# Decay attention's bias as two rows of the second score product, its mask in the reduction, and weights loaded into their final tiles, in a hybrid S5 / decay-attention layer

## The chip, the cores and the metric

The kernel runs on one core of one Trainium2 chip. The metric is the device time of one execution in microseconds (us), here the median of three executions; lower is better. TensorE is written PE, VectorE DVE, ScalarE ACT, GpSimd POOL and SyncE SP, as in the profile.

## What is computed

One layer of an encoder over 1024 positions of width 1024: an S5 state-space branch and a decay ("forgetting") attention of 8 heads x 64 side by side, one output projection and a residual; cross-attention to 256 memory tokens; a gated feed-forward. The change touches the decay attention and what follows it. Cut to that:

```python
cum_log_f = jnp.cumsum(jax.nn.log_sigmoid(f_logit), axis=1)          # per head and position
for blk in range(seq // 128):                                        # causal, 128 queries at a time
    q0, k_end = blk * 128, blk * 128 + 128
    s = jnp.einsum('bqhd,bkhd->bhqk', q[:, q0:k_end], k[:, :k_end]) / sqrt(64)
    s = jnp.where(q_pos[:, None] >= k_pos[None, :],
                  s + cum_log_f[q0:k_end, None] - cum_log_f[None, :k_end], -1e30)
    outs.append(softmax(s) @ v[:, :k_end])
x = x + rms_norm(concat(rms_norm(y_ssm), rms_norm(y_fox)) @ w_out)   # w_out: 512 rows for each branch
x = x + rms_norm(softmax(h @ wq @ k_mem.T / 16) @ v_mem @ wo)        # k_mem, v_mem = mem_n @ wkv
```

A row's softmax doesn't change when a constant is added to the row, so only the term of the key, `-cum_log_f[k]`, has to be added.

## The kernel before

Every large product is done as three products in the format fp32r: each operand is split in a high part (ACT rounds it, `split`, line 113) and a low part (DVE subtracts, line 115), and `mm3` (lines 121 to 124) multiplies high x high, high x low and low x high. Work is recorded by Python generators in stages; a scheduler then fixes one order for each engine, and each engine runs its list in that order. So an instruction that waits holds up all that stands behind it on its engine. That goes for SP too, which issues nearly all loads. Tiles come from pools with a fixed number of buffers (tag `a`: 2, `b`: 2, `c`: 3, `e`: 1, `t2`: 3, `raw`: 2, `whl`: 3, `slab`: 16), and a load into a buffer waits until the last reader of what was in it is done.

The stages around the change:

- **Input projections** (`in_proj`, line 869): keys, values, gates and queries, with the S5 recurrence on DVE between them. `qk_tile` writes queries and keys to DRAM (`qk_d`) as a high and a low half, `f_gate` (line 336) the running sum of the log gates (`nc_d`). The value tiles of the second half (`v1`) are spread between the S5 output steps `ssm_out` by the numbers in `V1_AT` (line 38). `ssm_out` (line 635) multiplies with tables `T` that SP loads from `T_d` (line 632).
- **Decay attention** (`fox`, line 705): 64 units, 8 heads x 8 blocks of 128 queries. `prepare` (line 709) loads for a head the query tile `qs` (64 high rows over 64 low rows), the keys `ka` (high keys in both halves of the rows, and low keys in both), and `ncb`, the running sum repeated over 128 partitions. `scores` (line 722) makes up to 1024 columns in a two-bank PSUM tile: for each 512 columns a product with the high keys (line 730) and one with the low keys (line 731), and on the last 128 columns a third one that adds the mask (line 733, a bf16 identity x `maskb`). One DVE instruction (line 737) adds `ncb` and takes the row minimum; ACT exponentiates (739), DVE divides by the row sum (740, 741). `turn` transposes the unit on PE (758), `values` multiplies with v (772). The scores run two units ahead.
- **Fillers** between the units, on the same engines: gated unit of S5 (`glu`), the S5 half of the output projection (`out_ssm`, line 818, to DRAM `t1_d`, which the trace calls t_d), memory keys and values (`mem_load` with `raw<-in_memT`, `mem_tile` with a weight `in_wkv` each, line 966), and the first key matrix of the cross-attention (`build_a`, line 993).
- **Output projection** (lines 1023 to 1082): the attention half of w_out is loaded in four pieces to `raw` and split to four slabs; then a loop over eight row blocks multiplies (PSUM tile x), adds the S5 half `t` (loaded at line 1063, line 1070), squares, normalises and adds x (loaded at 1060, line 1078). The value weights of the cross-attention (`value_weights`) are made between them.
- The cross-attention, the feed-forward (line 1294) and its last product (line 1557) follow.

Of the kernel before, what the change touches and what calls it, by code (L numbers as in the profile page):

```python
# [17 lines left out]
P = 128  # L18
S = 1024
# [18 lines left out]
V1_AT = (3, 1, 1, 1, 1)  # L38
# [14 lines left out]
def layer(ctx: ExitStack, tc: tile.TileContext, a, out):  # L53
# [35 lines left out]
    identb = const.tile([P, P], BF16, name="identb")  # L89
    dve.tensor_copy(identb, ident)  # L90
# [57 lines left out]
    boost = 5000  # L148
    stA, stB, stC = pool, pool, pool
# [4 lines left out]
    def load_w(src, shape, first=0, stage=None):  # L154
        w = tt(stage, [P, D]) if stage else raw([P, D])
        hl = whl([P, 2, D])
        if not first:
            sp.dma_start(out=w, in_=src)
# [23 lines left out]
    nc_d = dram.tile([NH, S], F32, name="nc_d")  # L182
    t1_d = dram.tile([L, NC, D], F32, name="t1_d")
    kv_d = dram.tile([16, P, 256], F32, name="kv_d")
    x1_d = dram.tile([NT, P, D], F32, name="x1_d")
# [150 lines left out]
    def f_gate(ftok):  # L336
        ps = s_ps([P, S])[0:NH]
        for j in range(NT):
            pe.transpose(ps[:, j * P:(j + 1) * P], ftok[:, j], ident)
        f, fl = ps, tt("a", [NH, S])  # L340
        dve.tensor_scalar(out=f, in0=ps, scalar1=fb, scalar2=None, op0=ALU.add)
        f = f.rearrange("p (j c) -> p c j", j=L)
        fc = fl.rearrange("p (c j) -> p c j", j=L)
        act.activation(out=fc, in_=f, func=AF.Abs)
        act.activation(out=fl, in_=fl, func=AF.Exp, scale=-1.0)
        act.activation(out=fl, in_=fl, func=AF.Ln, bias=1.0)
        dve.scalar_tensor_tensor(out=fc, in0=f, scalar=0.0, in1=fc, op0=ALU.min, op1=ALU.subtract)
        dve.tensor_tensor_scan(out=fl, data0=fl, data1=fl, initial=0.0, op0=ALU.add, op1=ALU.min)
        stA.dma_start(out=nc_d, in_=fl)
# [355 lines left out]
    def fox(yf):  # L705
# [3 lines left out]
        def prepare(h):  # L709
            r0 = (h % 2) * 64  # L710
            qs = tt("a", [P, S], F32R)
            ka = slab([P, 2, S])
            ncb = tt("b")
            sp.dma_start(out=ncb, in_=nc_d[h:h + 1, :].broadcast_to([P, S]))
            heads[h] = (qs, ka, ncb)
            q, k = qs.bitcast(F32), ka.bitcast(F32)
            for t in range(2):
                sp.dma_start(out=q[t * 64:t * 64 + 64], in_=qk_d[h // 2, t, r0:r0 + 64])
            for rr in (0, 64):
                sp.dma_start(out=k[rr:rr + 64], in_=qk_d[4 + h // 2, :, r0:r0 + 64].rearrange("t p s -> p t s"))  # L720

        def scores(h, t):
            qs, ka, ncb = heads[h]
            ke = (t + 1) * P
            ps = s_ps([P, S])
            qt = qs[:, t * P:(t + 1) * P]
            for c0 in range(0, ke, 512):
                c1 = min(ke, c0 + 512)
                dg = c1 == ke
                pe.matmul(ps[:, c0:c1], qt, ka[:, 0, c0:c1], start=True, stop=False)  # L730
                pe.matmul(ps[:, c0:c1], qt, ka[:, 1, c0:c1], start=False, stop=not dg)  # L731
                if dg:
                    pe.matmul(ps[:, ke - P:ke], identb, maskb, start=False, stop=True)
            sc = tt("c")
            nlr = sm(3, "nlr")
            nm, l, rl = (nlr[:, i:i + 1] for i in range(3))
            dve.tensor_tensor_reduce(out=sc[:, :ke], in0=ps[:, :ke], in1=ncb[:, :ke], scale=1.0,
                                     scalar=3e38, op0=ALU.add, op1=ALU.min, accum_out=nm)
# [294 lines left out]
    def value_weights(h):  # L1033
        vr = t2t([P, 2, 256])
        sp.dma_start(out=vr, in_=kv_d[8 + 2 * h:8 + 2 * h + 2].rearrange("d p m -> p d m"))
        vh = tt("bebe"[h], [P, 2, 2, 256], F32R)
        split(vh[:, 0], vh[:, 1], vr)
# [3 lines left out]
        for c in range(2):  # L1041
            tiles = [(mt, (x_ps if h == 3 else g_ps)([P, 512])) for mt in range(2)]
            for d in range(2):
                for mt, ps in tiles:
                    ms = slice(mt * P, mt * P + P)
                    mm3(ps, vh[:, 0, d, ms], vh[:, 1, d, ms], wo_[d][0][:, c], wo_[d][1][:, c], d == 0, d == 1)
# [10 lines left out]
    for n, j in enumerate((3, 4, 5, 6, 7, 0, 1, 2)):  # L1057
        ts = slice(j * P, (j + 1) * P)
        xt = tt("c")
        sp.dma_start(out=xt, in_=a["x"][ts, :])  # L1060
        t = tt("aab"[n % 3])
        for i in range(2):
            sp.dma_start(out=t[64 * i:64 * i + 64], in_=t1_d.rearrange("j (k s) d -> s k j d", s=16)[2 * j + i])
# [565 lines left out]
```

## Time and profile before

| | |
|---|---|
| median of 3 runs (lowest, highest) | 1413.33 us (1409.28, 1413.37) |
| profiled execution: its own time, its span | 1414.33 us, 1412.5 us |
| PE, DVE, ACT, POOL busy | 98%, 67%, 46%, 27% of the span |
| granted TensorE clock over the span | 0.992 |
| attention with its fillers | from 235.0 us (first score product) to 489.8 us (last value product starts) |
| output projection and start of the cross-attention | to about 560 us |

PE's busy time overlaps itself where matmuls are pipelined, so a share of busy time says little about how fast products follow each other. What is read below is the start of one product against the start of the next, the gaps in which PE has nothing running, and the granted clock of a stretch: PEclk 0.84 means that TensorE was granted 84% of its full clock in that stretch. Rows of waits name the engine that was late by the semaphore that came last.

### The profile page before, as it was taken

To read this page: it belongs to the slowest core of one execution; us is meant where nothing else is said; L and a number is where in the kernel's file an instruction comes from. 1 tells how busy PE (TensorE), PEld (TensorE's weight loads), DVE (VectorE), ACT (ScalarE), POOL (GpSimd) and SP (SyncE) were. 2 spreads that over 40 slices of the span, in tenths; PEclk is the share of its full clock that TensorE was granted. 3 is DMA by queue.
4 is the path that set the end of the run, shared out by engine and by line. 5 is a ranking of instruction groups with operands and counts; after the bars stand their busy time and mean duration, and the time that the engine had idled before them with its cause. 6 is when DMAs were issued, how large, how long until landed. Compare 5 with 4: busy or idle time off the path is not lost.

```text
span 1412.5 us, 20273 instructions
## 1 busy us (share of the span) xinstructions
PE 1381.8 (98%) x7353; PEld 1163.3 (82%) x7353; DVE 951.9 (67%) x1719; ACT 652.3 (46%) x1289; POOL 379.7 (27%) x430
## 2 busy tenths in 40 slices
PE   9999989999999899999999999999999999999997
PEld 7889889789889677888888788888888888888886
DVE  8949944857567668545467777877776676655566
ACT  7383345766566546433344533333333334544351
POOL 0011110011211043001021367676766661000021
PEclk9999999999999999999999999999999999999999
DMA  6235665267663665024467345554444447955544
GB/s 217 91 108 163 201 220 138 69 200 213 183 180 113 175 194 186 27 75 152 161 202 257 97 176 193 178 187 161 145 158 154 165 150 236 357 196 194 179 164 164
DMA packets 104501, 239.45 MB, mean 170 GB/s; under 512 B 11464, under 2 KB 40136, under 8 KB 104272
## 3 DMA queue, kind: packets, MB, share of 16 engines
q1 hardware_dynamic: 85872, 176.24, 40.0%
q0 software_dynamic: 18528, 61.91, 12.3%
q8 instruction: 58, 0.95, 0.3%
q14 instruction: 43, 0.35, 0.1%
HBM read 169.43 MB, written 77.33 MB: 175 GB/s over the span
## 4 chain that ended last, share of the span: by engine, by line
PE 84%; DVE 7%; issue 3%; DMA 3%; ACT 2%; POOL 0%; SPq 0%; DVEq 0%; ACTq 0%; POOLq 0%
PE x L1294 17%; PE g L1294 13%; PE x L1557 7%; PE g L1557 7%; PE g L122 7%; PE g L124 7%; PE g L123 7%; PE x L123 2%; PE x L124 2%; PE g L758 2%; PE x L122 2%; PE g L772 2%; PE s L730 1%; PE s L731 1%; DMA a<-t_d 1%
## 5 line engine op out<-in xcount | busy, mean ns | idle before, releaser
L1294 PE MATMUL x<-slab,op 128*128 128x512 f32 x984 | 233.2, 389 | 0.5 <-DVE op L115 0.5
L1294 PEld LDWEIGHTS x<-slab,op 128*128 128x128 f32 x984 | 184.7, 188 | 39.2 <-DVE op L115 1.0
L1294 PE MATMUL g<-slab,op 128*128 128x512 f32 x744 | 178.7, 389 | 0.0
L115 DVE TENSOR_TENSOR slab<-slab 128x1024 fp32r<-128x1024 f32 (+2 forms) x92 | 110.2, 1207 | 86.4 <-ACT slab L113 85.2
L1294 PEld LDWEIGHTS g<-slab,op 128*128 128x128 f32 x744 | 139.7, 188 | 29.0
L122 PE MATMUL g<-slab,whl 128*128 128x512 f32 (+1 forms) x416 | 151.4, 364 | 0.8 <-ACT slab L485 0.4
L124 PE MATMUL g<-slab,whl 128*128 128x512 f32 (+1 forms) x416 | 148.7, 358 | 0.0
L123 PE MATMUL g<-slab,whl 128*128 128x512 f32 (+1 forms) x416 | 148.3, 357 | 0.0
L113 ACT ACTIVATE slab<-slab 128x1024 fp32r<-128x1024 f32 (+2 forms) x92 | 94.7, 1036 | 108.6 <-DMA slab<-hs_d 80.8
L1557 PE MATMUL g<-slab 128*128 128x512 f32 x462 | 126.6, 389 | 0.0
L1557 PE MATMUL x<-slab 128*128 128x512 f32 x462 | 126.6, 389 | 0.0
L1557 PEld LDWEIGHTS g<-slab 128*128 128x128 f32 x462 | 86.7, 188 | 18.0
L1557 PEld LDWEIGHTS x<-slab 128*128 128x128 f32 x462 | 86.7, 188 | 18.0
L115 DVE TENSOR_TENSOR op<-slab,op 128x512 fp32r<-128x512 f32 x80 | 84.6, 1068 | 11.5 <-ACT op L113 11.3
L1370 POOL TENSOR_TENSOR wt<-wt 128x256 f32<-128x256 f32 x88 | 83.1, 944 | 21.0 <-DMA wt<-in_w_down 17.4
L122 PE MATMUL g<-whl,slab 128*128 128x256 f32 (+2 forms) x288 | 86.8, 310 | 1.7 <-ACT yt L318 0.7
L122 PEld LDWEIGHTS g<-slab,whl 128*128 128x128 f32 x416 | 78.6, 189 | 12.0 <-ACT whl L113 0.6
L124 PEld LDWEIGHTS g<-slab,whl 128*128 128x128 f32 x416 | 78.4, 189 | 11.6 <-DVE whl L115 0.2
L123 PEld LDWEIGHTS g<-slab,whl 128*128 128x128 f32 x416 | 78.6, 189 | 10.6
L113 ACT ACTIVATE op<-slab 128x512 fp32r<-128x512 f32 x80 | 50.0, 628 | 79.9 <-PE g L1294 38.0
L124 PE MATMUL g<-whl,slab 128*128 128x256 f32 (+2 forms) x288 | 86.0, 299 | 0.0
L123 PE MATMUL g<-whl,slab 128*128 128x256 f32 (+2 forms) x288 | 85.7, 298 | 0.0
(397 smaller groups left out, 2890.3 us busy)
## 6 DMA issues: line engine op xcount, KB each, us to landing
hs_d<-ev POOLq DMA_DIRECT2D x77, 256.0 KB, 2.6
slab<-hs_d SPq DMA_DIRECT2D x35, 512.0 KB
wt<-in_w_down SPq DMA_DIRECT2D x44, 256.0 KB
wt_d<-wt POOLq DMA_DIRECT2D x22, 512.0 KB, 5.1
slab<-in_w_gate SPq DMA_DIRECT2D x20, 512.0 KB
slab<-in_w_up SPq DMA_DIRECT2D x20, 512.0 KB
slab<-wt_d SPq DMA_DIRECT2D x20, 512.0 KB
wd_d<-in_w_down SPq DMA_DIRECT2D x33, 256.0 KB
```

Of the source, the lines that this page charges most:

```text
L113: first = act.activation(out=hi, in_=src, func=AF.Copy, scale=1.0 if mul is None else mul)
L115: (lo_eng or dve).tensor_tensor(out=lo, in0=src, in1=hi.bitcast(F32), op=ALU.subtract)
L122: pe.matmul(ps, lh, rh, start=first, stop=False)
L123: pe.matmul(ps, lh, rl, start=False, stop=False)
L124: pe.matmul(ps, ll, rh, start=False, stop=last)
L730: pe.matmul(ps[:, c0:c1], qt, ka[:, 0, c0:c1], start=True, stop=False)
L731: pe.matmul(ps[:, c0:c1], qt, ka[:, 1, c0:c1], start=False, stop=not dg)
L758: pe.transpose(tp[:, k], sc[:, (k0 + k) * P:(k0 + k + 1) * P], ident)
L772: pe.matmul(yp[hh * 64:hh * 64 + 64, c0:], w, pts[2 * hp + hh, qc][:, k, c0:], start=k == 0, stop=k == nk - 1, tile_position=(0, 64 * hh))
L1294: pe.matmul(ps, x[:, k], y[:, k], start=first and k + n == 0, stop=k == 3 and n == 2, skip_group_check=not first)
L1370: pool.tensor_tensor(out=o, in0=x, in1=y, op=ALU.subtract)
L1557: pe.matmul(banks[n][j], xo[:, u, js], wo[:, v], start=ends[0] and k == 0, stop=ends[1] and k == 2, skip_group_check=onto is not None)
```

## The change

Scores: `prepare` no longer loads `ncb` and no longer loads the low keys twice. It loads a second query tile `q1` of 66 rows, the 64 high query rows and two rows of ones (from a new DRAM tile `one_d`), and puts the high and the low part of the running sum (`nc_d`, now split in `f_gate`) in rows 64 and 65 of the low keys. The second score product then has 66 rows and adds the bias itself; the product of low queries with low keys is dropped. The mask product is gone: `maskb` is now 512 wide, zeros but for its last 128 columns, and is the addend of the DVE reduction, which is done for each 512 columns, so that units with over 512 columns have two reductions, the second starting from the minimum of the first.

Weights: the attention half of w_out is copied from its input to a DRAM tile `wof_d` early (behind the last key projection's weight) and later loaded from there straight into the low half of its slab, to be split in place; the memory keys (`build_a`) and values (`value_weights`) are loaded into the tile that their split writes. In the output loop `t` alternates between tags `a` and `b`, x goes to `e` or `c`, and the loads are recorded behind the one of the last w_out piece. `V1_AT` begins with 2 in place of 3.

```diff
-V1_AT = (3, 1, 1, 1, 1)
+V1_AT = (2, 1, 1, 1, 1)
...
-    maskb = const.tile([P, P], BF16, name="maskb")
+    maskb = const.tile([P, 512], BF16, name="maskb")
     pool.memset(maskb, 0.0)
-    pool.affine_select(out=maskb, in_=maskb, pattern=[[-1, P]], compare_op=ALU.is_ge,
+    pool.affine_select(out=maskb[:, 384:], in_=maskb[:, 384:], pattern=[[-1, P]], compare_op=ALU.is_ge,
...
-        stA.dma_start(out=nc_d, in_=fl)
+        for h in range(2):
+            hs = slice(h * 512, h * 512 + 512)
+            hi = t2t([NH, 512], F32R)
+            split(hi, fl.bitcast(F32R)[:, hs], fl[:, hs])
+            stA.dma_start(out=nc_d[:, 0, hs], in_=hi.bitcast(F32))
+        stA.dma_start(out=nc_d[:, 1], in_=fl)
+        one = tt("yt", [2, 256])
+        dve.memset(one, 1.0)
+        for i in range(4):
+            stA.dma_start(out=one_d[:, i * 256:i * 256 + 256], in_=one)
...
-            ncb = tt("b")
-            sp.dma_start(out=ncb, in_=nc_d[h:h + 1, :].broadcast_to([P, S]))
+            q1 = tt("b", [66, S], F32R)
...
-            for rr in (0, 64):
-                sp.dma_start(out=k[rr:rr + 64], in_=qk_d[4 + h // 2, :, r0:r0 + 64].rearrange("t p s -> p t s"))
+            sp.dma_start(out=k[0:64], in_=qk_d[4 + h // 2, :, r0:r0 + 64].rearrange("t p s -> p t s"))
+            sp.dma_start(out=k[64:128, 0], in_=qk_d[4 + h // 2, 0, r0:r0 + 64])
+            sp.dma_start(out=o[0:64], in_=qk_d[h // 2, 0, r0:r0 + 64])
+            sp.dma_start(out=o[64:66], in_=one_d)
+            sp.dma_start(out=k[64:66, 1], in_=nc_d[h])
...
-                pe.matmul(ps[:, c0:c1], qt, ka[:, 0, c0:c1], start=True, stop=False)
-                pe.matmul(ps[:, c0:c1], qt, ka[:, 1, c0:c1], start=False, stop=not dg)
-                if dg:
-                    pe.matmul(ps[:, ke - P:ke], identb, maskb, start=False, stop=True)
-            dve.tensor_tensor_reduce(out=sc[:, :ke], in0=ps[:, :ke], in1=ncb[:, :ke], scale=1.0,
-                                     scalar=3e38, op0=ALU.add, op1=ALU.min, accum_out=nm)
+                pe.matmul(ps[:, c0:c1], qs[:, ts], ka[:, 0, c0:c1], start=True, stop=False)
+                pe.matmul(ps[:, c0:c1], q1[:, ts], ka[0:66, 1, c0:c1], start=False, stop=True)
+                add = maskb[:, 512 - (c1 - c0):] if c1 == ke else maskb[:, 0:1].broadcast_to([P, 512])
+                dve.tensor_tensor_reduce(out=sc[:, c0:c1], in0=ps[:, c0:c1], in1=add, scale=1.0,
+                                         scalar=low if c0 else 3e38, op0=ALU.add, op1=ALU.min,
+                                         accum_out=nm if c1 == ke else low)
...
+            if i == 3:
+                with tc.issue_after(fetched[-1].ins):
+                    for j in range(4):
+                        sp.dma_start(out=wof_d[j], in_=a["w_out_f"][j])
...
-            kr = t2t([P, 2, 256])
+            kh = tt(("ea", "ba")[c][h], [P, 2, 2, 256], F32R)
+            kr = kh[:, 1].bitcast(F32)
             sp.dma_start(out=kr, in_=kv_d[2 * hd:2 * hd + 2].rearrange("d p m -> p d m"))
-            kh = tt(("ea", "ba")[c][h], [P, 2, 2, 256], F32R)
...
-        w = raw([P, D])
-        sp.dma_start(out=w, in_=a["w_out_f"][i])
         hl = slab([P, 2, D])
+        w = hl[:, 1].bitcast(F32)
+        wo_read = sp.dma_start(out=w, in_=wof_d[i])
...
-        vr = t2t([P, 2, 256])
+        vh, vl = t2t([P, 2, 256], F32R), t2t([P, 2, 256], F32R)
+        vr = vl.bitcast(F32)
...
-        xt = tt("c")
-        sp.dma_start(out=xt, in_=a["x"][ts, :])
-        t = tt("aab"[n % 3])
-        for i in range(2):
-            sp.dma_start(out=t[64 * i:64 * i + 64], in_=t1_d.rearrange("j (k s) d -> s k j d", s=16)[2 * j + i])
+        t = tt("ab"[n % 2])
+        with tc.issue_after(wo_read.ins) if n else ExitStack():
+            for i in range(2):
+                sp.dma_start(out=t[64 * i:64 * i + 64], in_=t1_d.rearrange("j (k s) d -> s k j d", s=16)[2 * j + i])
+        xt = tt("ec"[n % 4 > 0])
+        with tc.issue_after(wo_read.ins):
+            sp.dma_start(out=xt, in_=a["x"][ts, :])
```

The scheduler makes a new order from this. Three places of SP's list, on which steps of the prediction rest; the line numbers of the changed kernel are its own. **Place 1**, the tables of the S5 output and the first head's loads, before:

```order
L665 DMA raw<-in_glu_w 128x1024 x2
L632 DMA slab<-T_d 128x1024 x2
L718 DMA a<-qk_d 64x1024 x2
L714 DMA b<-nc_d 128x1024
L158 DMA raw<-in_w_out_s 128x1024
```

and in the changed kernel, where L642 loads the tables, L727 `qs` and L730 and L731 `q1`:

```order
L675 DMA raw<-in_glu_w 128x1024 x2
L727 DMA a<-qk_d 64x1024
L642 DMA slab<-T_d 128x1024 x2
L157 DMA raw<-in_w_out_s 128x1024
L730 DMA b<-qk_d 64x1024
L731 DMA b<-one_d 2x1024
```

The first query load now stands ahead of the tables of the first half; before, it stood behind them. On PE, 49 products of `v1` (three tiles begun) stood ahead of the first S5 output product, and now 34 (two tiles begun).

**Place 2**, the third and fourth head's loads and the first memory weights, before (L718 `qs`, L714 `ncb`, L720 `ka`, L158 a weight):

```order
L956 DMA raw<-in_memT 128x4x256 x2
L718 DMA a<-qk_d 64x1024 x2
L714 DMA b<-nc_d 128x1024
L720 DMA slab<-qk_d 64x2x1024 x2
L718 DMA a<-qk_d 64x1024 x2
L158 DMA raw<-in_wkv 128x1024
```

and now (L727 `qs`, L730 and L731 `q1`, L728, L729 and L732 `ka`):

```order
L971 DMA raw<-in_memT 128x4x256 x2
L727 DMA a<-qk_d 64x1024 x2
L730 DMA b<-qk_d 64x1024
L731 DMA b<-one_d 2x1024
L728 DMA slab<-qk_d 64x2x1024
L729 DMA slab<-qk_d 64x1024
L732 DMA slab<-nc_d 2x1024
L157 DMA raw<-in_wkv 128x1024 x2
L727 DMA a<-qk_d 64x1024 x2
```

The first two memory weights moved ahead of the fourth head's query load. **Place 3**, the start of the output projection, before (L1063 `t`, L1060 x, L1026 a piece of w_out):

```order
L1063 DMA a<-t_d 64x1x1024 x2
L1026 DMA raw<-in_w_out_f 128x1024
L1035 DMA t_6060<-kv_d 128x2x256
L1063 DMA b<-t_d 64x1x1024 x2
L1060 DMA c<-in_x 128x1024 x2
L1026 DMA raw<-in_w_out_f 128x1024 x2
```

and now (L1077 `t`, L1042 the pieces of w_out, L1080 x):

```order
L1077 DMA a<-t_d 64x1x1024 x2
L1042 DMA slab<-wof_d 128x1024 x4
L1080 DMA e<-in_x 128x1024
L1077 DMA b<-t_d 64x1x1024 x2
L1080 DMA c<-in_x 128x1024 x2
```

The four pieces now stand together behind the first `t`, and three more `t` follow them without a weight of w_out between; before, the first piece stood ahead of all this, and the last two behind the third `t`. From the first key transposes of the cross-attention on, PE's order is the same in both.

More of the change, by code (lines that the diff above doesn't have):

```diff
@@ L148, in layer @@
     boost = 5000
+    fetched = []
     stA, stB, stC = pool, pool, pool
@@ L157, in load_w @@
         if not first:
-            sp.dma_start(out=w, in_=src)
+            fetched.append(sp.dma_start(out=w, in_=src))
         for cs in (slice(0, first), slice(first, D)):
@@ L722, in scores @@
+            sp.dma_start(out=k[64:128, 0], in_=qk_d[4 + h // 2, 0, r0:r0 + 64])
+            sp.dma_start(out=o[0:64], in_=qk_d[h // 2, 0, r0:r0 + 64])
+            sp.dma_start(out=o[64:66], in_=one_d)
+            sp.dma_start(out=k[64:66, 1], in_=nc_d[h])
         def scores(h, t):
-            qs, ka, ncb = heads[h]
+            qs, q1, ka = heads[h]
             ke = (t + 1) * P
             ps = s_ps([P, S])
-            qt = qs[:, t * P:(t + 1) * P]
+            ts = slice(t * P, (t + 1) * P)
@@ L727, in scores @@
+            sc = tt("c")
+            nlr = sm(4, "nlr")
+            nm, l, rl, low = (nlr[:, i:i + 1] for i in range(4))
             for c0 in range(0, ke, 512):
                 c1 = min(ke, c0 + 512)
-                dg = c1 == ke
-                pe.matmul(ps[:, c0:c1], qt, ka[:, 0, c0:c1], start=True, stop=False)
-                pe.matmul(ps[:, c0:c1], qt, ka[:, 1, c0:c1], start=False, stop=not dg)
-                if dg:
-                    pe.matmul(ps[:, ke - P:ke], identb, maskb, start=False, stop=True)
```

18 lines of the change are left out of this document (7 added, 11 removed).

## The prediction

> **What bounds the kernel now.** I read the page of the profile first: busy shares, granted clock, the chain that ended last.
>
> ```profile
> PE 1381.8 (98%) x7353; PEld 1163.3 (82%) x7353; DVE 951.9 (67%) x1719; ACT 652.3 (46%) x1289; POOL 379.7 (27%) x430
> PEclk9999999999999999999999999999999999999999
> PE 84%; DVE 7%; issue 3%; DMA 3%; ACT 2%; POOL 0%; SPq 0%; DVEq 0%; ACTq 0%; POOLq 0%
> ```
>
> PE is nearly always busy and carries 84% of the chain that ended last. Time can go in two ways only: fewer products, or fewer stretches in which PE waits. The other 16% of the chain says where to look, so the second view was busy time and clock by stretch (PE, PEld, DVE, ACT and POOL busy with instruction counts, then granted clock, DMA share, GB/s). I cut it at the stretches in which gaps of PE lie near the change, and added the long one behind them.
>
> ```profile
> 188.00:210.00 22.00, 17.64 (x125) 17.05 (x125) 3.87 (x5) 7.71 (x12) 3.22 (x6) 0.84 0.78 256
> 264.00:294.00 30.00, 24.96 (x172) 21.10 (x171) 23.54 (x61) 22.17 (x51) 1.45 (x2) 0.89 0.35 105
> 460.00:492.00 32.00, 27.92 (x193) 21.54 (x192) 19.70 (x35) 16.98 (x33) 3.45 (x3) 0.95 0.69 183
> 519.00:557.00 38.00, 33.23 (x140) 25.51 (x139) 29.92 (x52) 20.91 (x66) 15.66 (x13) 0.96 0.68 223
> 560.00:765.00 205.00, 204.40 (x1018) 170.87 (x1016) 113.55 (x283) 86.04 (x221) 23.23 (x34) 1.00 0.41 131
> ```
>
> PE idles 22.00 - 17.64 = 4.4 us in the first stretch, 5.0 in the second, 4.1 in the third and 4.8 in the fourth, together 18.3. The clock costs as much again in part: (1 - 0.84) x 22 = 3.5, (1 - 0.89) x 30 = 3.3, 1.6 and 1.5, together 9.9. So about 28 us of the span are waits near the change and their slow clock. From 560 us on PE is full (204.40 of 205) and its order is unchanged, so what is saved earlier should come through to the end.
>
> **The change part by part.** The sum is made against the profiled execution, 1414.3 us, which is 1.0 above the median of 1413.3.
>
> *The mask product.* Each unit loses one, 64 in all. The timeline of PE has it twice in different company (start, duration, line):
>
> ```profile
> 235.38 0.23 PE L733 MATMUL s<-maskb,identb 128*128 128x128 bf16 x1
> 235.42 0.37 PE L730 MATMUL s<-slab,a 128*128 128x256 f32 x1
> ...
> 238.79 0.23 PE L733 MATMUL s<-maskb,identb 128*128 128x128 bf16 x1
> 238.85 0.28 PE L758 MATMUL g<-ident,c 128*128 128x128 f32 x1
> ```
>
> Its 0.23 us overlap with the next product; what it takes of PE is the step to the next start, 0.04 and 0.06 us. 64 x 0.055 = 3.5 us, between 64 x 0.04 = 2.6 and, one hundredth more than the larger for its place among weight loads, 64 x 0.07 = 4.5. PE is the bound here, so all of it counts: **-3.5**. The second product keeps its columns; I cost its 66 rows in place of 128 at nothing, since it streams as many columns (the opposite is a rival below).
>
> *The reduction on DVE.* 32 units (four blocks of each head) have over 512 columns and now two reductions each. By form:
>
> ```profile
> L737 DVE CUSTOM_DVE_ANT_0 c<-s,b 128x1024 f32<-128x1024 f32 x8 | 9.8, 1220 | 2.2 <-PE g L758 1.7 <-PE s L733 0.5
> ...
> L737 DVE CUSTOM_DVE_ANT_0 c<-s,b 128x512 f32<-128x512 f32 x8 | 5.5, 687 | 1.3 <-PE s L733 1.2
> ...
> L737 DVE DVE_READ_ACCUMULATOR2_ANT nlr<- 128x1 f32 x64 | 5.3, 83 | 0.0
> ```
>
> Two of 512 columns and their two reads of the accumulator take 2 x (0.687 + 0.083) = 1.54, one of 1024 took 1.30: 0.24 more, 32 x 0.24 = 7.6 us of DVE. Against it, the first half can be reduced while PE makes the second. The view by stretch has the cover:
>
> ```profile
> 270.00:470.00 200.00, 193.65 (x1552) 172.01 (x1550) 135.42 (x321) 127.75 (x279) 28.26 (x41) 0.98 0.59 165
> 150.00:160.00 10.00, 10.00 (x46) 8.26 (x45) 9.50 (x27) 2.37 (x4) 2.14 (x4) 1.00 0.66 191
> ```
>
> DVE has 200 - 135.4 = 65 us free over most of the attention, and the scores run two units ahead. So **0**; without that cover it is 7.6, and more in the third rival. The split of the running sum adds two subtractions of 512 columns, by the 512 row about 2 x 0.69 = 1.4 us, on a DVE that is full about then (9.50 of 10) while PE is full too (10.00): 0 to 1.4, taken at 0 and held in the bounds of the next step. The reads for the heads (seven smaller transfers for five, no repeated rows) and the copy of w_out inside DRAM go by SP long before they are needed: 0.
>
> *First memory weights, 264 to 294 us.* The chain of waits there:
>
> ```profile
> 280.12 0.47 SPq L718
> 280.63 0.60 SPq L718
> 281.32 4.87 DMA raw<-in_wkv
> 286.22 1.06 ACT whl L113
> ```
>
> The weight stood behind the fourth head's query load, which waited for its buffer until PE had read it at 280.12; then ACT split the weight, from 286.22 on, before it came to what PE stood waiting for. Now the first two weights stand ahead of that load. Their buffers and the DMA engines are free (DMA share 0.35 in this stretch, 0.01 in 270 to 280), so the 4.87 us of the load lie beside products. The loss was 5.0 + 3.3 = 8.3; half stays, since DVE and ACT are nearly full just before (9.96 and 8.82 of 10): **-4.3**, between 0 and -7.
>
> *S5 output, 188 to 210 us.* SP's timeline, then PE's:
>
> ```profile
> 183.40 1.14 SPq L632 DMA_DIRECT2D slab<-T_d  x2
> 187.27 1.14 SPq L718 DMA_DIRECT2D a<-qk_d  x2
> 189.57 1.15 SPq L632 DMA_DIRECT2D slab<-T_d  x2
> ```
> ```profile
> 190.23 0.28 PE L122 MATMUL g<-whl,slab 128*128 128x256 f32 x1
> 190.35 0.39 PE L643 MATMUL g<-slab 128*128 128x128 f32 x2
> ...
> 198.60 0.80 PE L643 MATMUL g<-slab 128*128 128x128 f32 x2 [3.33 <-ACT t L316]
> ```
>
> The first tables were asked for at 183.40. Now a query load stands ahead of them, and that one was not free to go before 187.27. The tables would go out at about 187.9 and, if they take the 4 to 5 us of the weight above, land near 192. PE has 15 products of `v1` fewer ahead, at 0.12 each (190.23 to 190.35) 1.8 us, and would be at the tables at 188.5: a new wait of about 3. The old wait of 3.33, for ACT, ends when it did; PE comes to it 192 - 190.35 = 1.7 later, and 1.8 later still if the 15 products stand before it, so I leave 0.5 of it. With 1.7 for the clock (half of the 3.5 that this stretch loses now) the new loss is 3 + 1.7 + 0.5 = 5.2, against 4.4 + 3.5 = 7.9: **-2.7**, between 0 and -5.
>
> Does a wait of that length cost clock? In the row of this stretch the longest gap is 3.33 us and the clock is 0.84; shorter gaps did it too:
>
> ```profile
> 270.00:280.00 10.00, 9.50 (x61) 8.57 (x59) 9.96 (x31) 8.82 (x21) 0.00 (x0) 0.83 0.01 2
> ```
>
> Here PE idles 0.5 us of 10 and has 0.83. I keep the 1.7. The Trainium skill, "TensorE: Matmul & The Clock Gate", Part 1, says the clock halves after at least one idle window of about 3.4 us; by it a wait of 3 us would cost no clock, and the time would be 1.7 lower. The row just quoted doesn't agree with that, if idle means that no product runs.
>
> *w_out of the attention half, 460 to 492 us.* The chain there:
>
> ```profile
> 475.84 8.49 DMA raw<-in_w_out_f
> 484.41 1.07 ACT slab L113
> 485.50 1.24 DVE slab L115
> ```
>
> and the first `t` in SP's timeline:
>
> ```profile
> 461.61 1.30 SPq L1063 DMA_DIRECT2D a<-t_d  x2
> ```
>
> The last two pieces waited behind the third `t`, and landed after 8.5 us. Now the four pieces stand together, behind the first `t` alone, which went out at 461.61. They are 2 MB; at this stretch's 183 GB/s that is about 11 us, so they land near 473, and the output products start without them only when attention ends earlier than that. The 4.1 + 1.6 = 5.7 lost would become about 1.2, the two splits behind each other; but slabs are to be free for all four at once, and the value loads move behind. **-2.0**, between +3 and -5.
>
> *The output loop, 519 to 557 us.* The chain:
>
> ```profile
> 512.07 2.17 DVE c L1078
> 514.25 0.59 SPq L1063
> 514.89 7.52 DMA a<-t_d
> ...
> 532.69 7.37 DMA a<-t_d
> ```
>
> A `t` was asked for when a buffer came free (by DVE's last step, 512.07) and took 7.5 us to land, twice on the chain. Before, two of three `t` went to the two buffers of tag `a`; now they go over the four of `a` and `b` in turn, and x to `e` and `c`, so each `t` can be asked for a row block earlier. 4.8 + 1.5 = 6.3 are lost now; DVE, 29.92 of 38 busy, will not allow all: **-3.5**, between 0 and -6.
>
> A new order also makes waits that the old one doesn't have; I put **+3** for them, a sixth of the 18.3 us that PE idles now, with 0 to 6 as its bounds; no row of the profile before can show them. The sum: -3.5 - 2.7 - 4.3 - 2.0 - 3.5 + 3 = -13.0, and 1414.3 - 13.0 = 1401.3, forecast **1401**.
>
> **The rivals.** *The waits only move.* PE runs one list; if what was late is followed by something about as late (the splits on ACT and DVE, the tables), only the mask product's 3.5 stays: 1414.3 - 3.5 = 1410.8, or 1408 if one wait goes. For it: ACT and DVE at 8.8 and 9.96 of 10 ahead of the second stretch. Against: three of the four waits are for transfers that are now asked for earlier.
>
> *The halved reduction holds DVE up: slower.* DVE takes its list in order. Where it comes to a reduction before PE has made the scores, it stands, and all behind it (splits, divisions, evictions) with it. The waits of DVE in the attention:
>
> ```profile
> DVE c L737 <- PE s L733: 11.8, 11, 1.8
> DVE c L737 <- PE g L758: 3.2, 4, 0.9
> ```
>
> That is 15.0 us for 64 reductions, 0.23 each. 32 more at that price are 7.5, with the 7.6 busy 15.1. If the waits for loads only move, the 3.5 of the mask product are all there is against it: it decides once over 3.5 lie on PE's path. With half, 1414.3 - 3.5 + 7.6 = 1418; with all, 1426. Against it: the 65 us that DVE has free.
>
> *The bias is not free: 66 rows.* That the second product makes a bias at no cost fails if PE takes longer for 66 rows over two row halves. The step of a 512 column product is 0.23 us:
>
> ```profile
> 238.38 0.39 PE L731 MATMUL s<-slab,a 128*128 128x512 f32 x1
> 238.61 0.22 PE L730 MATMUL s<-slab,a 128*128 128x128 f32 x1
> ```
>
> A head has 128 x (1 + ... + 8) = 4608 columns, nine times 512; 72 x 0.23 = 16.6 us for all. Twice as long would give 1401.3 + 16.6 = 1418. No row that I quote has such a product. The Trainium skill, same page, Part 2, has it that loading weights takes time by their columns and that the rows don't matter, which speaks against this rival; no run here shows it yet.
>
> **How the numbers follow.** The forecast has 0.64, the moved waits 0.20, the held-up DVE 0.10, the 66 rows 0.06. About 0.3% (4.2 us) is what a measurement of this kernel can tell from no change. The forecast lies wholly below 1409.1. Of the moved waits, at 1408 to 1411, I give 0.07 to faster and 0.13 to no change; of the 66 rows, at 1418 with the base 1.0 above the median, 0.03 each to no change and slower. So faster 0.71, same 0.16, slower 0.10 + 0.03 = 0.13. All terms at their best are -4.5 - 5 - 7 - 5 - 6 = -27.5, or 1387; that all are is not likely, so the range begins at 1389. It ends at 1415, above the moved waits, and leaves out the two slower cases with 0.16.
>
> **What would show it.** In the changed profile PE's busy time over the span falls little and its idle time in these four stretches falls from 18 us to about 10. The weights of the memory keys should be issued near 271 to 275 and the chain should not go through them; the four pieces of w_out should be issued between 460 and 470 in one row; the tables of the S5 output should be issued at 187 to 188, and PE should wait for them, which would show the first term right though it is a loss in itself. The steps between products of 512 columns should be 0.23 still. The prediction is wrong if DVE's waits for the scores grow past 20 us, or if PE's idle time is as before with other releasers.

## The result: slower, and the profile after

| | before | changed |
|---|---|---|
| median (lowest, highest) | 1409.87 us (1405.75, 1413.37), 5 runs | 1419.47 us (1415.59, 1422.19), 5 runs |
| profiled execution, span | 1412.5 us | 1417.7 us |

The ratio is 1.0063, 95% interval 1.0039 to 1.0088. The forecast was 1401 us with a range of 1389 to 1415, so the sign was wrong and the range missed. The three runs shown before the prediction were among the slower of the five of the kernel before; its median is now 3.5 us lower. The two profiled executions lie 5.1 us apart (1414.33 and 1419.47), the medians 9.6, so the traces show a part of the loss only. Ratios are of executions that ran alike: a single one of 5486.73 us, in experiment 11, is left out of them.

The page of the changed kernel. PE has 64 products fewer and is busy for 2.2 us less, and the span is 5.2 us longer:

```profile
PE 1379.6 (97%) x7289; PEld 1161.3 (82%) x7289; DVE 957.4 (68%) x1785; ACT 652.1 (46%) x1291; POOL 382.3 (27%) x436
PEclk9999999899999998999999999999999999999999
```

The same stretches as in the prediction, and one more (228 to 242) in which a loss is new:

```profile
188.00:210.00 22.00, 17.94 (x151) 17.21 (x149) 7.28 (x9) 10.68 (x18) 3.23 (x6) 1.00 0.81 257
228.00:242.00 14.00, 12.20 (x61) 9.78 (x60) 7.85 (x23) 7.37 (x17) 1.08 (x2) 0.88 0.55 161
264.00:294.00 30.00, 27.35 (x170) 23.53 (x169) 24.33 (x71) 22.03 (x51) 1.45 (x2) 0.83 0.28 79
460.00:492.00 32.00, 28.24 (x197) 22.02 (x196) 23.70 (x44) 19.68 (x38) 3.07 (x4) 0.95 0.74 205
519.00:557.00 38.00, 28.21 (x118) 22.90 (x117) 26.35 (x45) 16.27 (x55) 16.76 (x13) 0.87 0.62 196
560.00:765.00 205.00, 203.67 (x1025) 170.87 (x1024) 114.68 (x280) 88.24 (x225) 22.73 (x33) 1.00 0.39 125
```

Add the idle time of PE to what the clock takes, as the prediction did. The S5 output lost 7.9 us before and now 4.1. The memory weights lost 8.3 and now 2.65 + 5.1 = 7.8. The w_out stretch lost 5.7 and now 3.8 + 1.6 = 5.4. The output loop lost 6.3 and now 9.8 + 4.9 = 14.7. The new place at 228 to 242 loses 1.8 + 1.7 = 3.5, where the kernel before loses 0.2. So 8.4 us more are lost in the output loop alone: 5.0 are idle time and 3.4 clock, with one gap of PE of 9.79 us in it. In PE's timeline the bracket at a row's end is the idle time before it and who ended it:

```profile
542.37 0.39 PE L122 MATMUL g<-whl,t 128*128 128x512 f32 x1
552.55 0.80 PE L120 MATMUL g<-whl,t 128*128 128x512 f32 x1 [9.79 <-ACT t L111]
```

What ACT was late for is read backwards, in the timelines of SP, ACT and DVE:

```profile
532.69 0.38 SPq L1015 DMA_DIRECT2D a<-kv_d  x1
537.39 0.33 SPq L1080 DMA_DIRECT2D c<-in_x  x1
546.32 0.38 SPq L1015 DMA_DIRECT2D b<-kv_d  x1
548.52 0.33 SPq L157 DMA_DIRECT2D raw<-in_wqT  x1
548.95 0.39 SPq L1051 DMA_DIRECT2D t<-kv_d  x1
```
```profile
542.58 0.63 ACT L111 ACTIVATE a<-a 128x512 fp32r<-128x512 f32 x1 [7.65 <-DMA a<-kv_d]
```
```profile
543.24 0.69 DVE L113 TENSOR_TENSOR a<-a 128x512 fp32r<-128x512 f32 x1 [7.93 <-ACT a L111]
...
545.01 1.28 DVE L1095 SCALAR_TENSOR_TENSOR c<-b,r,c 128x1024 f32<-128x1024 f32 x1
```

A key tile of the cross-attention is now loaded straight into the tile of tag `a` that its split fills, and that buffer was held by the loop's `t` until 532.7 (SP waited 3.4 us there for DVE's last step of the row block). The load took 9.9 us from issue to use, with about 2.5 MB of x, t and weights asked for in the 9 us ahead of it. ACT stood in front of that split for 7.65 us and DVE for 7.93, and both take their lists in order. So the row block that holds a buffer of tag `b` was finished only at 546.3 (545.01 + 1.28). The second key load on SP waited for exactly that buffer, and the value tile stood behind it: asked for at 548.95, split, in use at 552.55. In the kernel before the key lay in a `t2` tile by then, and only its split waited for the buffer, as the chain of waits has it:

```profile
540.84 1.28 DVE c L1078
542.15 0.64 ACT b L113
542.82 1.03 DVE b L115
```

There the split starts 0.03 us after the buffer came free (540.84 + 1.28 = 542.12). The change put a DMA of 10 us into that place.

### The profile page after: what moved, and what is told of

Same layout as the page of the kernel before. It is cut to its first block, busy times and chain, and to the rows that moved or that the text cites. A ratio compares the mean times of both kernels' runs of the same rounds, so it can differ in the third digit from the quotient of the medians.

```text
span 1417.7 us, 20287 instructions
## 1 busy us (share of the span) xinstructions
PE 1379.6 (97%) x7289; PEld 1161.3 (82%) x7289; DVE 957.4 (68%) x1785; ACT 652.1 (46%) x1291; POOL 382.3 (27%) x436
## 4 chain that ended last, share of the span: by engine, by line
PE 59%; DVE 0%; ACT 0%; DMA 0%; issue 0%; DVEq 0%; ACTq 0%
PE x L1311 17%; PE g L1311 13%; PE x L1574 7%; PE g L1574 7%; PE g L122 2%; PE g L120 2%; PE g L121 2%; PE x L120 2%; PE x L122 2%; PE x L121 2%; PE g L1107 1%; PE g L1218 1%; DVE whl L113 0%; DMA raw<-in_wqT 0%; ACT whl L111 0%
## 5 line engine op out<-in xcount | busy, mean ns | idle before, releaser
L113 DVE TENSOR_TENSOR slab<-slab 128x1024 fp32r<-128x1024 f32 (+2 forms) x96 | 115.8, 1214 | 87.0 <-ACT slab L111 85.3
L111 ACT ACTIVATE slab<-slab 128x1024 fp32r<-128x1024 f32 (+2 forms) x96 | 99.3, 1039 | 108.8 <-DMA slab<-hs_d 76.0
L113 DVE TENSOR_TENSOR op<-slab,op 128x512 fp32r<-128x512 f32 x80 | 87.5, 1104 | 12.0 <-ACT op L111 11.7
```

What stands on the lines that cost most here:

```text
L111: first = act.activation(out=hi, in_=src, func=AF.Copy, scale=1.0 if mul is None else mul)
L113: (lo_eng or dve).tensor_tensor(out=lo, in0=src, in1=hi.bitcast(F32), op=ALU.subtract)
```

## The experiments

Theory K: the key load, bound to a buffer which the output loop holds, costs the time. Rival S: the scores part (halved reductions, smaller loads) does. All ratios are against the kernel before, run on the same chip alongside.

**1. Keys through t2 again.**

```diff
-            kh = tt(("ea", "ba")[c][h], [P, 2, 2, 256], F32R)
-            kr = kh[:, 1].bitcast(F32)
+            kr = t2t([P, 2, 256])
             sp.dma_start(out=kr, in_=kv_d[2 * hd:2 * hd + 2].rearrange("d p m -> p d m"))
+            kh = tt(("ea", "ba")[c][h], [P, 2, 2, 256], F32R)
```

> The changed kernel, with the four key tiles of the cross-attention loaded to a tile of tag t2 and split from there, as before the change. Theory K (the 9.8 us gap of PE at 542.8 us comes from the key load that now has to wait for the last reader of its buffer of tag a, and whose landing ACT and DVE then wait for in order): the gap is gone, idle time of PE in 519 to 557 falls from 9.8 to about 5 us, half-clock stretches there from 10.2 to 3.4 us; 7 to 10 us faster than the changed kernel, ratio to the kernel before 0.998 to 1.002. Rival S (the halved reductions and the new head loads cost the time): the gap may go, the time stays within 3 us of the changed kernel, ratio 1.004 to 1.008.

Measured: 1409.06 us, ratio 0.9973 (0.9961 to 0.9986). That is 0.9% or some 13 us under the changed kernel; what is left of the change is faster than the kernel before. The output loop, in the view by stretch:

```profile
519.00:557.00 38.00, 34.25 (x173) 28.09 (x172) 32.73 (x61) 23.28 (x68) 15.83 (x12) 1.00 0.72 224
```

3.75 us of PE idle in place of 9.79, and no half clock. Theory K holds; the gain is larger than its forecast (7 to 10 us, 0.998 to 1.002).

**2. The scores part alone,** on the kernel before (the diff of `prepare`, `scores`, `f_gate` and `maskb` as in the change).

> The kernel before with the scores part of the change alone: bias as two rows, mask as addend of the reduction, split running sum. Weights, output loop and V1_AT as before. Theory K: the mask product's 3.5 us come off, waits move by a few us; 0 to 7 us faster, ratio 0.995 to 1.000. Rival S: 5 to 10 us slower, ratio 1.004 to 1.007, with DVE's waits for scores above 15 us.

Measured: 1418.39 us, ratio 1.0048 (1.0030 to 1.0065). Rival S gets the number, and its sign is there: DVE's waits for scores are 23.7 us, 15.0 before, and PE waits 4.6 us for DVE's reductions and quotients in the attention, 0.7 before. Theory K's forecast for this run is wrong. The longest single wait of PE has another releaser, though:

```profile
488.53 0.69 PE L781 MATMUL g<-slab 128*64 128x256 f32 x2 [6.36 <-ACT slab L772]
```
```profile
471.44 2.17 SPq L1035 DMA_DIRECT2D raw<-in_w_out_f  x2
```
```profile
485.71 1.06 ACT L111 ACTIVATE slab<-raw 128x1024 fp32r<-128x1024 f32 x1 [10.90 <-DMA raw<-in_w_out_f]
```

The last two pieces of w_out are asked for at 471.44, 4.4 us earlier than before the change (475.84), and still land later: ACT splits them from 485.71 on, before from 484.41. The copy that PE needs (L772) stands behind these splits on ACT, and PE, which gets there earlier, stands in front of it for 6.36 us in place of 1.54. The output loop loses more too: 6.7 us idle at a clock of 0.90, where it was 4.8 at 0.96. How the 0.48% divides among these is not shown.

**3. The weights part alone** (scores as before, everything else changed).

> The changed kernel with the scores part undone (bias from a repeated row by DVE, mask as third product, running sum whole), so that weights loaded in place, output loop and V1_AT are what is left of the change. Theory K: the gap of 8 to 11 us near the end of the output loop is there, and the mask product isn't saved: ratio 1.006 to 1.011. Rival S: within 0.3% of the kernel before.

Measured: 1417.45 us, ratio 1.0034 (1.0020 to 1.0048). The gap is there, by the same path (ACT stands 10.2 us for the key load of tag `a`), without any of the scores edits. The whole is less than K's 1.006 to 1.011; the smaller gaps of PE at the S5 output (1.56 and 0.56 us, not 2.50 and 0.61) are about 1 us of that, and the rest is open:

```profile
547.06 0.79 PE L122 MATMUL g<-whl,t 128*128 128x512 f32 x1 [10.80 <-ACT t L113]
```

**4. The output loop's loads as before** (t in tags a, a, b; x in c; not held behind w_out), all else changed.

> The changed kernel with the output loop's loads as before (t in tags a, a, b, x in tag c, none of them recorded behind the last piece of w_out); keys, values and w_out still loaded in place. Theory K, if the buffer of tag a is late because the loop's t tiles hold it: the key load's wait stays as long as t goes through tag a, the gap is 5 to 11 us and the ratio 1.003 to 1.009. Rival L (the new alternation of t and x is what delays the loads): the gap is gone, ratio 0.996 to 1.002.

Measured: 1420.62 us, ratio 1.0058 (1.0041 to 1.0074). The number is in theory K's range, but not for its reason. The gap near 542 is gone (rival L's sign: the longest gap of PE left there is 2.1 us), and another one has come, for the pieces of w_out, which now stand behind t and x on SP:

```profile
487.59 1.65 PE L120 MATMUL x<-slab 128*128 128x512 f32 x3 [7.82 <-ACT slab L111]
```
```profile
486.48 1.06 ACT L111 ACTIVATE slab<-slab 128x1024 fp32r<-128x1024 f32 x1 [10.07 <-DMA slab<-wof_d]
```

So the order of the loop's loads is worth its place, and the 9.8 us gap takes both edits: the key in place and t over both tags.

**5. Weights part without the keys.** Experiment 1 with the scores part undone.

> The changed kernel with the scores part undone and the keys through tag t2 again: what is left is w_out through its slab, the values in place, the loop's loads and V1_AT. It stands to the run with keys through t2 (0.9973) as the weights alone do to the whole change. Theory M (the scores part gains the mask product's 3.5 us): 0.999 to 1.001, slower than 0.9973. Rival D (the halved reductions give back as much or more in waits of PE for DVE): 0.992 to 0.997, with no wait of PE for the divided scores between 294 and 460 us.

Measured: 1410.28 us, ratio 0.9987 (0.9971 to 1.0003), between the two forecasts; rival D's sign is there (no wait of PE for divided scores between 294 and 460). With the scores part it was 0.9973: the scores part gains 0.14% or 2 us in this company, where the intervals overlap, and loses 0.48% in experiment 2's. Against experiment 3 it tells what the keys in place cost with the old scores and all other weights edits: 0.9987 to 1.0034, 0.47% or 6.6 us, half of the 0.9% of experiment 1; why half is open.

**6. One reduction for each unit,** keys through t2.

```diff
-    maskb = const.tile([P, 512], BF16, name="maskb")
+    maskb = const.tile([P, S], mybir.dt.int8, name="maskb")
...
-                add = maskb[:, 512 - (c1 - c0):] if c1 == ke else maskb[:, 0:1].broadcast_to([P, 512])
-                dve.tensor_tensor_reduce(out=sc[:, c0:c1], in0=ps[:, c0:c1], in1=add, scale=1.0,
-                                         scalar=low if c0 else 3e38, op0=ALU.add, op1=ALU.min,
-                                         accum_out=nm if c1 == ke else low)
+            dve.tensor_tensor_reduce(out=sc[:, :ke], in0=ps[:, :ke], in1=maskb[:, S - ke:].bitcast(mybir.dt.uint8),
+                                     scale=1.0, scalar=3e38, op0=ALU.add, op1=ALU.min, accum_out=nm)
```

> The changed kernel with the keys through t2, and one reduction for each unit in place of one for each 512 columns: the mask is a tile of 1024 bytes a row (0, and 255 where masked), read as the addend. It leaves the bias rows and the dropped mask product as they are. Rival D (the halving costs): 2 to 5 us faster than with two reductions, ratio 0.9940 to 0.9960, DVE's reads of the accumulator in the scores fall from 96 to 64 and PE waits for divided scores under 1 us. Theory M (halving is free since DVE has time): 0.9965 to 0.9980.

Measured: 1405.46 us, ratio 0.9955 (0.9937 to 0.9974), against 0.9973 (0.9961 to 0.9986) with two: rival D's number, 2.5 us, with intervals that overlap. Rival D's signs are there: 64 reads of the accumulator for 96, and under 1 us of waits for divided scores. Waits of the changed kernel in 230 to 475 us (total, times, longest), PE's and DVE's:

```profile
PE g L769 <- DVE c L752: 2.7, 6, 0.9
PE s L744 <- DVE nlr L747: 2.5, 4, 1.4
```
```profile
DVE c L747 <- PE s L745: 19.3, 26, 2.3
DVE c L747 <- PE g L769: 6.0, 7, 1.3
```

and with one reduction:

```profile
PE s L744 <- DVE nlr L746: 2.1, 1, 2.1
PE g L767 <- DVE c L750: 0.7, 1, 0.7
```
```profile
DVE c L746 <- PE s L745: 12.1, 14, 2.7
DVE c L746 <- PE g L767: 5.9, 8, 1.4
```

DVE's waits for scores were 15.0 us before the change, 25.3 in it, and are 18.0 here; PE waits 0.7 for divided scores and not 2.7, and 2.1 for a free score tile (`s`), not 2.5. The fair comparison is experiment 1, which has the same keys and two reductions: DVE waits 26.4 there, PE 1.7 and 2.5. So PE's waits for DVE's scores fall by 1.4 us of 4.2, and the time by 2.5 us that the intervals do not tell from nothing.

**7. Keys in place, but in two tiles of tag t2** and not in one of e, a or b.

```diff
-            kh = tt(("ea", "ba")[c][h], [P, 2, 2, 256], F32R)
-            kr = kh[:, 1].bitcast(F32)
+            kh, kl = t2t([P, 2, 256], F32R), t2t([P, 2, 256], F32R)
+            kr = kl.bitcast(F32)
```

> The changed kernel with the keys still loaded in place, into the tile that their low half ends in, but in two tiles of tag t2 and not in one of tag e, a or b. Theory K, sharper: it is the buffer shared with the loop's t and x that is late, so the gap of 9.8 us at 542 is gone: ratio 0.996 to 1.000. Rival P (a load in place is late wherever it goes, since it can't be sent before the tile is free): a gap of 5 us or more stays, ratio 1.003 to 1.008.

Measured: 1413.16 us, ratio 1.0017 (1.0003 to 1.0030), between the forecasts. The gap near 542 is gone: no gap of PE is longer than 1.7 us from 470 to 575. So the buffer shared with the loop is what made the 9.8 us, and half of the loss with it. The other half of the way to 0.9973 stays: the last key is asked for at 558.86, where it was 547.61 in experiment 1. Here a key holds two of the three buffers of t2, which the values use as well, and one in experiment 1; that this is all of the other half is not shown.

**8. The mask product twice** (kernel before, line 733 issued twice).

> The kernel before with each of the 64 mask products issued twice (the mask is added twice). It prices the term of the mask product. By the step of 0.04 to 0.07 us in the trace: 2.6 to 4.5 us slower, ratio 1.0018 to 1.0032. Rival: PE starts so small a product in time that it has anyway: ratio 0.999 to 1.001.

Measured: 1412.79 us, ratio 1.0008 (0.9992 to 1.0023), or 1.1 us with -1.1 to 3.2. PE's timeline has what two of them take, 241.01 to 241.10:

```profile
241.01 0.23 PE L733 MATMUL s<-maskb,identb 128*128 128x128 bf16 x1
241.08 0.22 PE L734 MATMUL s<-maskb,identb 128*128 128x128 bf16 x1
241.10 0.48 PE L122 MATMUL g<-slab,whl 128*128 128x512 f32 x1
```

Steps of 0.07 and 0.02 us. Of the forecast of 2.6 to 4.5 us the interval leaves 2.6 to 3.2, and it leaves the rival's nothing as well. The order was made anew for this kernel too, and its PE idles 20.9 us in all where the kernel before idles 22.2 (sums of all gaps in PE's timeline), so what 64 products take by themselves isn't settled closer.

**9. Tables ahead of the query load,** on top of experiment 6.

```diff
+            with ExitStack() if h else tc.issue_after(T_read[1].ins):
                 for t in range(2):
                     sp.dma_start(out=q[t * 64:t * 64 + 64], in_=qk_d[h // 2, t, r0:r0 + 64])
```

> The run with one reduction (0.9955), with one more edit: the first head's query loads are put behind the first two tables of the S5 output on SP, as before the change. Theory A (the new wait of PE at 189 us, 2.6 us there, is for tables that stand behind a query load whose buffer isn't free yet): the tables are asked for at 183 and not at 187, the wait falls under 1 us and the time by 1 to 3 us, ratio 0.9930 to 0.9950. Rival: the wait is given back at the next wait for ACT near 195 to 199: ratio 0.9950 to 0.9965, with a gap of 2 us or more at 195 to 199.

Measured: 1402.69 us, ratio 0.9948 (0.9928 to 0.9968), no difference from experiment 6 that can be told. The ratio lies in theory A's range, but its signs are not there, and theory A falls: the order on SP is the wanted one, the tables are asked for at 186.06 and not at 183, and the wait is still 2.30 us. Nor is there the rival's gap of 2 us at 195 to 199.

```profile
186.06 0.80 SPq L643 DMA_DIRECT2D slab<-T_d  x2
187.05 1.14 SPq L729 DMA_DIRECT2D a<-qk_d  x2
```
```profile
189.98 0.46 PE L654 MATMUL g<-slab 128*128 128x128 f32 x2 [2.30 <-DMA slab<-T_d]
```

SP's waits name the cause, DVE's last step (L635) in making the S5 states ahead of the output:

```profile
SPq L643 <- DVE b L635: 6.0, 2, 4.9
```

In the changed kernel both were late at once: SP stood 4.6 us for the query load's buffer, until 186.34, and 0.9 more for DVE. Without the scores part (experiment 3) the tables are asked for at 182.95, and before the change at 183.40. That DVE is late by some 3 us because the running sum is split on it while it is full fits this, but no run here tried the split alone.

**10. V1_AT with 3 again,** on top of experiment 6.

> The run with one reduction (0.9955), with V1_AT beginning with 3 as before the change. It tells the two edits near 190 us apart. If the move of the third value tile behind the first S5 products is what removed the wait for ACT of 3.3 us and its half clock: that wait is back, 2 to 5 us slower, ratio 0.9970 to 0.9995. If the late tables alone did (PE comes later to the same place): the wait stays away, and PE waits less for the tables, ratio 0.9945 to 0.9960.

Measured: 1404.09 us, ratio 0.9949 (0.9931 to 0.9968). The wait for ACT is back as the first case has it, and the time isn't:

```profile
192.85 0.46 PE L653 MATMUL g<-slab 128*128 128x128 f32 x2 [0.97 <-DMA slab<-T_d]
199.68 0.79 PE L653 MATMUL g<-slab 128*128 128x128 f32 x2 [3.02 <-ACT t L317]
```

So the edit of V1_AT is what moves that wait, and it is worth nothing that these runs can tell.

**11. w_out and the loop as before,** on top of experiment 6.

> The run with one reduction (0.9955), with the attention half of w_out through tag raw as before, no copy in DRAM, and the output loop's loads as before. Theory W (the w_out part is what takes PE's wait near 482 us away, 6.4 us in the run with the scores part alone): the wait is back with 3 to 8 us and the ratio 0.9985 to 1.0030. Rival: that wait came from the halved reductions, and with one reduction it stays under 2 us: ratio 0.9945 to 0.9975.

Measured: 1415.40 us, ratio 1.0026 (1.0010 to 1.0043). Theory W has the number: w_out through its slab with the loop's loads is worth 0.7%, about 10 us, beside the new scores. Its profiled execution took 1410.05 us, 5 under the median, so its trace shows only part of where; PE's idle time there, 2.5 us at 489 and 3.8 at 515, is not at the place that W named.

**12. The key tiles in place, alone,** on the kernel before.

> The kernel before with the four key tiles loaded in place (tags e, a, b, a) and nothing else of the change. Theory K in its first form (a key load bound to a buffer of the output loop is late by itself): a wait of 5 us or more in 519 to 560, ratio 1.003 to 1.008. Second form (it takes the new alternation of t over a and b as well): the wait there is as before, ratio 0.998 to 1.002.

Measured: 1423.11 us, ratio 1.0097 (1.0073 to 1.0120): the first form and beyond it, though the longest single wait in the loop is 3.51 us and not 5. The first key tile, far from the output loop, pays as well, for PE waits for an instruction of ACT (L836) that stands behind the key's split; PE and ACT:

```profile
371.00 0.39 PE L122 MATMUL g<-whl,slab 128*128 128x256 f32 x1 [3.34 <-ACT t L836]
```
```profile
369.47 0.63 ACT L113 ACTIVATE e<-e 128x512 fp32r<-128x512 f32 x1 [6.70 <-DMA e<-kv_d]
```

So the second form, which said that it takes the new alternation as well, fails: the new alternation is not needed for the loss. The profiled execution, 1418.21 us, was the fastest of six and 4.9 under the median, so its trace shows only part of the 0.97%.

## Why the prediction was wrong, by its own steps

**The step that failed** is one that isn't in the sum. The change loads the keys of the cross-attention into the tile that their split fills, and the part by part had no term for it: not for the buffer that the load now waits for, not for ACT and DVE, which stand in order before its split, not for the value load behind it on SP. All that covered it was "+3 for waits of a new order, 0 to 6". Measured, it is 0.9% (changed kernel against experiment 1) and 0.97% (experiment 12 against the kernel before), 13 to 14 us, and 0.47% or 6.6 us with the old scores and the new weights (experiment 3 against 5).

**What is left without it** is 0.27% or 3.8 us of gain, where 13.0 were forecast. So the term that was missing has the sign, and the other terms together were still over three times too large. Idle time of PE plus what the clock takes, in us:

| stretch | before | changed | experiment 1 |
|---|---|---|---|
| 188 to 210, S5 output | 7.9 | 4.1 | 5.7 |
| 228 to 242 | 0.2 | 3.5 | 3.5 |
| 264 to 294, memory weights | 8.3 | 7.8 | 7.8 |
| 294 to 460, attention | 0 | 2.7 | 1.8 |
| 460 to 492, w_out | 5.7 | 5.4 | 3.0 |
| 519 to 557, output loop | 6.3 | 14.7 | 3.8 |
| sum | 28.4 | 38.2 | 25.6 |

The last two columns lie 12.6 us apart, which is the 0.9% of experiment 1.

With the keys through t2 the S5 output, w_out and the loop gain 2.2, 2.7 and 2.5 us, near their forecasts of 2.7, 2.0 and 3.5. The memory weights gain 0.5 for 4.3, and the new waits, at 228 to 242 and in the attention, take 5.1 for the 3 that the prediction allowed. Its sign, 18 us of idle time in its four stretches falling to about 10, reads 20.3 in the changed kernel and 13.4 in experiment 1.

**Mask product, -3.5.** Right in sign by the timeline, not confirmed by the time: experiment 8 has 1.1 us, from -1.1 to 3.2, which leaves out 3.5.

**Reduction on DVE, 0.** The reductions and their reads take 9.5 us more in the attention, for 7.6 worked out, since a second reduction takes longer (last section). That DVE's 65 us of free time hide them was too simple: free time in the mean doesn't help a list in order, and PE's waits for DVE's scores and their quotients went from 0.7 to 5.2 us in the attention. So the mechanism of the second rival (DVE held up; the prediction calls it the third in one place) was there. Its price is not settled: one reduction gives 2.5 us, a sixth of the rival's 15.1, with intervals that overlap. The prediction's own alarm, DVE's waits over 20 us, went off at 25.3; it does not tell slow from fast, since experiment 1, faster than the kernel before, has 26.4.

**66 rows.** Right. The products with 66 rows, and those with 128, in the changed kernel:

```profile
268.13 0.40 PE L744 MATMUL s<-slab,a 128*128 128x512 f32 x1
268.36 0.40 PE L745 MATMUL s<-slab,b 66*128 66x512 f32 x1
268.60 0.38 PE L769 MATMUL g<-ident,c 128*128 128x128 f32 x2
```

0.23 and 0.24 us apart: no price for fewer rows. The Trainium skill, "TensorE: Matmul & The Clock Gate", Part 2, says that the row count doesn't matter for loading weights; this trace agrees (the weight loads of these two products take 195 and 194 ns in the mean).

**S5 output, -2.7.** The new wait of about 3 came (2.50 us at 188.8, for the tables), and the old one for ACT went; without a half clock the stretch gained 3.8. The reason was half of it: the query load did hold the tables up, but without it they wait for DVE until about the same time (experiment 9). At 228 to 242, 3.3 us are new; whether that is this gain paid back is not shown.

**Memory weights, -4.3.** Only 0.5 came: idle time fell from 5.0 to 2.65, and the clock took 5.1 for 3.3. The step that failed is "Their buffers and the DMA engines are free". The weights stand earlier in SP's list, but were asked for at 282.50, later than before (281.32) and far from the 271 to 275 that was to show the gain. Both buffers of tag `raw` were taken by `raw<-in_memT`, and SP waited until DVE had split the last part of the first one (SP's waits from 262 to 290, then the timelines of DVE and SP):

```profile
SPq L157 <- DVE slab L115: 19.5, 1, 19.5
```
```profile
282.00 0.48 DVE L115 SCALAR_TENSOR_TENSOR slab<-raw,gains,slab 128x256 fp32r<-128x256 f32 x1
```
```profile
282.50 0.37 SPq L157 DMA_DIRECT2D raw<-in_wkv  x1
```

PE does not wait for that load any more; 2.2 of its 2.65 us are waits for score tiles that DVE's reductions free.

**w_out, -2.0, and loop, -3.5.** Together worth more than forecast beside the new scores (10 us, experiment 11); without the new scores, the whole weights part but for the keys is worth 1.8 us, with an interval that includes none (experiment 5). In the changed kernel the loop's gain was lost under the key's wait, which made it +8.4. The pieces of w_out stood in one row, as forecast, but went out from 469.3 to 476.8 and not between 460 and 470: the first `t` itself went out at 467.94 (461.61 before), and among the pieces SP waited 5.7 us for a slab that PE was still reading.

## What to carry to other kernels

A load in place saves a tile, but it binds the start of a transfer to the end of the buffer's last reader; a staging tile lets the transfer run early and leaves only the split behind the buffer. Before taking one away, look up who holds the final tile, and what stands behind the split on each in-order engine and behind the load on its queue. And price every edit in the diff, also those that look like housekeeping: the sum is worth no more than the term that isn't in it. Nor do parts add up: the scores alone lose 0.48%, the weights without the keys gain 0.13%, and both together gain 0.27%.

The best version found is the change with the keys through t2 and one reduction for each unit (0.9955), with or without the tables first (0.9948): about 6 to 7 us faster than the kernel before and 15 to 16 faster than the change.

## What of the hardware was not expected

- The clock is no simple matter of a gap's length. In the changed kernel the gap of 2.50 us at 188.8 cost no clock (1.00 in its stretch), while gaps of at most 1.4 us from 273 to 282 came with a granted clock of 0.83 over 30 us (0.50 from 275.8 to 285.9). By the Trainium skill, "TensorE: Matmul & The Clock Gate", Part 1, it takes an idle window of about 3.4 us; the second stretch does not agree with that, if idle means that nothing runs.
- A reduction that starts from a value in a tile takes longer than one that starts from a constant, with the same columns:

```profile
L747 DVE CUSTOM_DVE_ANT_0 c<-s,maskb 128x512 f32<-128x512 f32 x40 | 27.5, 688 | 12.1 <-PE g L769 6.0 <-PE s L745 5.3
...
L747 DVE CUSTOM_DVE_ANT_0 c<-s,maskb,nlr 128x512 f32<-128x512 f32 x8 | 6.0, 744 | 2.0 <-PE s L745 2.0
```

744 against 688 ns. The rows of 128 columns, all with the same addend, have 349 against 283. The addend's type and its repeated column made no difference (687 ns before, with f32).
